# Head sums by column halves, 64x64 products on four quadrants, and new distances in an RWKV-7 recurrence

## The chip, the cores and the metric

The kernel runs on one NeuronCore of one Trainium2 chip. Its time is the time on the device in microseconds (us); three runs are summed up by their median. The core's engines work on their own and wait for each other by semaphores: TensorE (PE) multiplies matrices, VectorE (DVE) and ScalarE (ACT) do elementwise work, GpSimd (POOL) a little of it, and SyncE (SP) issues most DMAs. PE reads from SBUF, which has 128 partitions, and writes to PSUM. PSUM has eight banks here, each of 128 partitions by 512 fp32 numbers; DVE or ACT must empty a bank before it is used again. A product takes its weights from partitions (the rows of PE's array) and leaves its result on partitions that belong to the array's columns. A product of 64x64 weights uses one quadrant of the array: a row half, given by the partition half of its inputs, and a column half, given by the partition half of its output.

## What is computed

One layer of a decoder: 1024 tokens of width 1024, all in float32. Cut to what the change touches:

```python
h = rms_norm(x)
z = h @ W_in
A = dilated_window_attention(q, k, v)          # 8 heads x 64
R = rwkv7(r, k, v, ...)                        # 8 heads x 64
x = x + rms_norm(concat[A, R] @ W_out)
x = x + rms_norm(relu(rms_norm(x) @ W_up)**2 @ W_down)

# in rwkv7, for each head
kk = k * k_k
kk = kk / max(sqrt(sum(kk * kk)), 1e-12)       # sum over the 64 numbers of a head
b = kk * a
for t in range(1024):
    sa = state @ kk[t]
    state = state * w[t] - outer(sa, b[t]) + outer(v[t], k[t])
    y[t] = state @ r[t]
bonus = sum(r * k * r_k) * v                   # sum over a head again
out = (group_norm(y) + bonus) * g
```

## The kernel before

The recurrence is worked in chunks of 64 tokens, so that most of it becomes products. Eight heads are four pairs, p = 0 to 3; a pair's two heads lie on the two partition halves (`own[0]`, `own[1]`). Sixteen chunks are handled as two halves f of eight. Inside a chunk the state's update is a triangular system, and its inverse is built per pair:

- `norms` (L379) sums the squares of each head of k: `pst`, eight products per pair of a 128x128 tile with `bone`, the two columns that mark the heads.
- `pre_pair` (L400) spreads the norms (`pn`, transposes), scales by the decay (`kk`, `ar`, `bk`, `km`), and forms the products `pN` of bk and ar (L433 to L436), one bank of tag "w" for each f. One DVE multiply by a mask empties it into N (L437). `pb` (L453) sums the bonus over heads, in the form of `pst`. The diagonal 16x16 blocks of N go through DRAM.
- `subst` (L478) inverts these blocks on DVE.
- `merge` (L496) combines them to 64x64 in two steps. Step one: `qu1` = N times X, copied to W by ACT (L511), then `qu2` = W times Z, copied into Z by DVE where a mask says so (L519), and a transpose (L520). Each of the two is 32 products per pair. Step two, `qu3` and `qu4`, does the like with 32x32 products.

Then eight units n of two chunks each run through all heads: `unit_ab` (products p of tag "w" and transposes ptk, banks "a" and "b"), `unit_e` (E, banks "a" and "b"), and `unit_c`, the loop over chunks that can't be broken. There, O gets 16 products with the state HV, ACT copies VU out of O (L635), O gets 16 products with VU, DVE adds HV (L641) and scales it for the next chunk (L642). `unit_g` is the group norm and gate of a unit; its operand bv comes by DMA.

Beside these run the input projections, tiles z_*: three matmuls per step, 24 steps for each half of a slab of 128 columns. Those of attention's last pair (z_aq, z_ak and z_av of p = 3) are allowed only after "C7", the recurrence's end. `gate` computes g (three matmuls, then an ACT copy), eight tiles that also use tag "w".

What sets the order: the planner `drive` runs while the program is built. Each job is a generator that, step by step, yields (PE cost, delay, label, needs). The planner's clock `now` counts PE cost. When a job's delay is over and its needs are met, its step is emitted; when no job is due, one filler step of three projection matmuls is emitted, at 0.7. The table `WAIT` (L31) overrides the delay of a job's start or of one of its steps by name (`mrg0.0` is the first step of merge of pair 0, `pre1.2` the third of pre_pair of pair 1, and so on). The order of PE and of SP is fixed by what comes out; the order on ACT and DVE is chosen by a scheduler by priorities and readiness. After the recurrence follow attention, W_out and the FFN.

The helpers that the change uses: `mm` is one matmul, and `mm_h` two, by column halves of the weights:

```python
for s_ in range(2):
    last = mm(o[64 * s_:64 * s_ + 64], lhsT[:, 64 * s_:64 * s_ + 64], rhs, start, stop)
```

## Time and profile before

| what | value |
|---|---|
| runs | 1335.83, 1336.62, 1343.36 us |
| median | 1336.62 us |
| span of the profiled execution | 1340.4 us |
| PE busy | 1279.0 us |
| DVE busy | 905.0 us |
| ACT busy | 625.9 us |
| recurrence's preparation and units on PE | about 80 to 440 us of the span |

The profiled execution has no time of its own beside its span; the span lies 3.8 us above the median. PE is the busiest engine over the whole span. In the rows of a timeline a number is the start, the next the duration of a group of equal instructions; what stands in brackets is the idle time of that engine ahead of it and what ended that. In the rows of stretches come the stretch, its length, the busy time of each engine with its count of instructions, the granted clock of PE (1.00 is full), and the share and rate of DMA. The granted clock is a measured number of the trace.

### The profile page before, as it was taken

What the parts mean: (1) busy time and instruction counts of PE and PEld (TensorE: products, weight loads), DVE (VectorE), ACT (ScalarE), POOL (GpSimd) and SP (SyncE); (2) the same over time, 40 slices, a digit from 0 to 9 for tenths busy, and PEclk for the clock granted to TensorE, in tenths of its full rate; (3) what the DMA queues carried; (4) which work ended last, traced back from release to release, by engine and by line L of the source; (5) the groups of instructions that cost most, each with busy time, mean ns of one, the idle gap of its engine ahead of it and who ended that gap; (6) DMA issues with size and microseconds to landing.
All of it is one profiled execution on the core that took longest, in us unless ns stands there. A gap on an engine that the chain in (4) does not pass through costs nothing.

```text
span 1340.4 us, 23558 instructions
## 1 busy us (share of the span) xinstructions
PE 1279.0 (95%) x9360; PEld 1057.7 (79%) x9360; DVE 905.0 (68%) x1647; ACT 625.9 (47%) x1026; POOL 36.2 (3%) x56
## 2 busy tenths in 40 slices
PE   6899999999889979999998999999999999999997
PEld 5687888888777868787886888888888888888875
DVE  7867668632778457554889977667766775446586
ACT  7653334233545267664656443434444444443442
POOL 0000000000000000000000000000000002000210
PEclk9999999999989989999999999999999999999999
DMA  7346756976774686503434454454457984345564
GB/s 259 116 173 174 189 138 170 257 206 215 218 233 150 204 249 189 139 25 96 142 109 143 171 171 146 141 165 156 151 182 246 348 321 166 95 140 191 188 211 166
DMA packets 163757, 239.48 MB, mean 179 GB/s; under 512 B 52192, under 2 KB 89312, under 8 KB 163648
## 3 DMA queue, kind: packets, MB, share of 16 engines
q1 hardware_dynamic: 154304, 212.81, 50.5%
q10 hardware_dynamic: 8064, 20.98, 4.6%
q0 software_dynamic: 1280, 4.20, 0.8%
q8 instruction: 73, 1.20, 0.4%
q14 instruction: 36, 0.29, 0.1%
HBM read 160.85 MB, written 77.09 MB: 178 GB/s over the span
## 4 chain that ended last, share of the span: by engine, by line
PE 75%; DVE 10%; DMA 7%; ACT 4%; issue 2%; SPq 1%; DVEq 0%; ACTq 0%
PE X L47 12%; PE dX L47 9%; PE Z L47 6%; PE pm L47 5%; PE dZ L47 5%; PE dY L47 3%; PE z_aq L47 3%; PE Y L47 3%; PE z_r L47 3%; PE z_v L47 3%; PE z_k L47 3%; PE z_av L47 3%; PE z_ak L47 2%; PE pS L47 2%; PE pT L908 2%
## 5 line engine op out<-in xcount | busy, mean ns | idle before, releaser
L47 PE MATMUL dX<-wow,wou 128*128 128x512 f32 x768 | 175.9, 390 | 2.7 <-DVE wow L1178 2.2
L47 PEld LDWEIGHTS dX<-wow,wou 128*128 128x128 f32 x768 | 143.8, 188 | 34.1 <-DVE wow L1178 3.5
L47 PE MATMUL dZ<-wow,wou 128*128 128x512 f32 x384 | 87.4, 389 | 0.0
L1177 ACT ACTIVATE wow<-wd 128x1024 fp32r<-128x1024 f32 x40 | 42.3, 1059 | 89.7 <-PE dZ L47 29.8
L47 PEld LDWEIGHTS dZ<-wow,wou 128*128 128x128 f32 x384 | 72.1, 188 | 15.0
L1178 DVE TENSOR_TENSOR wou<-ur,wou 128x1024 fp32r<-128x1024 f32 x56 | 72.0, 1287 | 6.9 <-ACT wou L1177 6.7
L1178 DVE TENSOR_TENSOR wow<-wd,wow 128x1024 fp32r<-128x1024 f32 x40 | 49.9, 1250 | 35.0 <-ACT wow L1177 34.8
L1177 ACT ACTIVATE wou<-ur 128x1024 fp32r<-128x1024 f32 x56 | 58.5, 1049 | 19.8 <-DMA ur<-u_d 12.4
L896 DVE CUSTOM_DVE_ANT_0 S<-pS,stripT 128x512 f32<-128x512 f32 (+3 forms) x64 | 37.6, 588 | 38.7 <-PE pS L47 19.7
L898 ACT ACTIVATE S<-S,mn 128x128 f32<-128x128 f32 (+7 forms) x64 | 49.3, 771 | 19.7 <-DVE mn L896 19.1
L1265 ACT ACTIVATE r<-u 128x512 f32<-128x512 f32 x48 | 30.0, 626 | 51.4 <-DVE u L1263 51.0
L908 PE MATMUL pT<-cst,S 128*128 128x128 f32 x288 | 43.7, 278 | 8.3 <-ACT PT L910 5.4
L47 PE MATMUL pm<-WO,mxr 128*128 128x512 f32 x192 | 49.1, 400 | 0.8 <-DVE mxr L976 0.8
L47 PE MATMUL pm<-WO,mxa 128*128 128x512 f32 x192 | 47.3, 403 | 0.0
L1178 DVE TENSOR_TENSOR wow<-TK,wow 128x1024 fp32r<-128x1024 f32 x16 | 20.8, 1301 | 38.9 <-ACT wow L1177 38.9
L47 PE MATMUL Z<-HB,wo 128*128 128x512 f32 x192 | 46.1, 389 | 0.0
L47 PE MATMUL z_aq<-hT,wh_aq 128*128 128x512 f32 x128 | 45.5, 407 | 0.0
L47 PE MATMUL X<-HB,wo 128*128 128x512 f32 x180 | 43.6, 390 | 1.6 <-ACT HB L1038 1.6
L47 PE MATMUL z_av<-hT,wh_av 128*128 128x512 f32 x128 | 45.2, 409 | 0.0
L908 PEld LDWEIGHTS pT<-cst,S 128*128 128x128 f32 x288 | 32.4, 140 | 16.0 <-ACT PT L910 10.5
L47 PE MATMUL z_k<-hT,wh_k 128*128 128x512 f32 x128 | 42.6, 395 | 1.4 <-DVE z L234 1.4
L47 PE MATMUL z_ak<-hT,wh_ak 128*128 128x512 f32 x128 | 43.7, 404 | 0.0
(388 smaller groups left out, 3060.6 us busy)
## 6 DMA issues: line engine op xcount, KB each, us to landing
ur<-u_d SPq DMA_DIRECT2D x56, 512.0 KB, 4.4
wd<-in_wdown_dram SPq DMA_DIRECT2D x40, 512.0 KB, 4.3
u_d<-S SPq DMA_DIRECT2D x64, 256.0 KB, 2.0
u_d<-u SPq DMA_DIRECT2D x48, 256.0 KB, 2.1
wr_upa<-in_wup_dram SPq DMA_DIRECT2D x16, 512.0 KB, 3.6
wr_upb<-in_wup_dram SPq DMA_DIRECT2D x16, 512.0 KB, 4.0
TK<-in_wdown_dram SPq DMA_DIRECT2D x16, 512.0 KB, 7.1
x<-in_x_dram SPq DMA_DIRECT2D x8, 512.0 KB, 7.0
```

What stands on the lines that cost most here:

```text
L47: return PE.matmul(o, lhsT, rhs, start=start, stop=stop, skip_group_check=True)
L896: V.tensor_tensor_reduce(Sx[:, lo:hi], pS[:, :hi - lo], stripT[:, so:so + hi - lo], 1.0, 3e38 if k == 0 else mn[:, 0:1], OP.add, OP.min, a ...
L898: A.activation(Sx[:, :w], Sx[:, :w], AF.Exp, scale=-1.0, bias=mn[:, nbk - 1:nbk], accum_out=at[p, "den"][:, i, h:h + 1])
L908: PE.transpose(pt[:, j], Sx[:, (4 * k + j) * P:(4 * k + j + 1) * P], ident)
L1177: A.activation(w[:, 0, 0:n], raw, AF.Copy)
L1178: E.tensor_tensor(w[:, 1, 0:n], raw, w[:, 0, 0:n].bitcast(F32), OP.subtract)
L1265: A.activation(r, src, AF.Relu)
```

## The change

It has three parts. First, the head sums `pst` and `pb` are computed by column halves (`mm_h`): 16 products of 128x64 weights per pair in place of 8 of 128x128. Second, the 64x64 products `pN`, `qu1` and `qu2` go to four quadrants by the new helper `turned`: results of even chunks stay on the partition half of their inputs (bank r = 0), those of odd chunks go to the other half (bank r = 1). The number of products stays. Each step's banks are now divided by the parity of the chunk instead of by f; `pN` takes both banks of tag "w" for each f, where it took one. The results are brought back to their places on the way out of PSUM (`sides`), by three operations: one for the even chunks, one for each half of the odd ones. Third, the steps' costs and delays in the planner and the table `WAIT` are set anew, so the order on PE and SP changes.

```diff
-WAIT = {'mrg1.0': 26.0, 'mrg1.3': 4.0, ..., 'vo0_1': 18.5, ..., 'VU3': 5.5, ..., 'EO1_1': 1, ...}
+WAIT = {'mrg1.0': 26.0, 'mrg1.3': 4.5, ..., 'vo0_1': 12.5, ..., 'VU3': 8.0, ..., 'EO1_1': 5.0, ..., 'norm0': 0, ..., 'pre0.2': 1.0, ...}
 ...
-                    mm(pst[:, 8 * f + 2 * t:8 * f + 2 * t + 2], sq[:, t * P:(t + 1) * P], bone)
+                    mm_h(pst[:, 8 * f + 2 * t:8 * f + 2 * t + 2], sq[:, t * P:(t + 1) * P], bone)
 ...
-            yield 2.0, 4.0
+            yield 1.2, 4.0
+
+        sides = [(slice(0, P), slice(0, P), 0), (lo, hi, 1), (hi, lo, 1)]
+
+        def turned(pq, f, lhsT, rhs):
+
+            for cc in range(0, 8, 2):
+                for r in range(2):
+                    for h in range(2):
+                        mm(pq[r][own[h ^ r], 4 * f + cc // 2], lhsT[own[h], cc + r], rhs[own[h], cc + r])
 ...
-                pN = bank(f"pN{p}_{f}", "w", bufs=2)
-                for cc in range(8):
-                    for h in range(2):
-                        mm(pN[own[h], cc], bk[own[h], cc, 0, :], ar[own[h], cc, 0, :])
-                V.tensor_tensor(N[:, 8 * f:8 * f + 8], pN, maskn.unsqueeze(1).to_broadcast([P, 8, 64]), OP.mult)
-                yield 1.0, (3.0, 2.5)[f]
+                pN = [bank(f"pN{p}_{f}_{r}", "w", (P, 4, 64), 2) for r in range(2)]
+                turned(pN, 0, bk[:, :, 0], ar[:, :, 0])
+                Nf = N[:, 8 * f:8 * f + 8]
+                for d, s_, r in sides:
+                    V.tensor_tensor(Nf[d, r::2], pN[r][s_], maskn[s_].unsqueeze(1).to_broadcast([s_.stop - s_.start, 4, 64]), OP.mult)
+                yield 0.7, (3.2, 2.7)[f]
 ...
-                    mm(pb[:, 8 * f + 2 * t:8 * f + 2 * t + 2], T[f][3][:, t * P:(t + 1) * P], bone)
+                    mm_h(pb[:, 8 * f + 2 * t:8 * f + 2 * t + 2], T[f][3][:, t * P:(t + 1) * P], bone)
             V.tensor_copy(BON[:, :, p, :], pb[:, 0:16].rearrange("p (t h) -> p t h", h=2))
-            yield 1.8, 1.0, f"B{p}"
+            yield 1.1, 1.0, f"B{p}"
 ...
+            pq = [bank(f"qu1_{p}_{r}", "bc"[r]) for r in range(2)]
             for f in range(2):
-                fs = slice(8 * f, 8 * f + 8)
-                pu = bank(f"qu1_{p}_{f}", "bc"[f])
-                for cc in range(8):
-                    for h in (0, 64):
-                        mm(pu[h:h + 64, cc], N[h:h + 64, 8 * f + cc], X[h:h + 64, 8 * f + cc])
-                A.activation(W[:, fs], pu, AF.Copy)
-            yield 2.4, 1.5
+                turned(pq, f, N[:, 8 * f:8 * f + 8], X[:, 8 * f:8 * f + 8])
+            for d, s_, r in sides:
+                A.activation(W[d, r::2], pq[r][s_], AF.Copy)
+            yield 1.3, 2.6
+            pq = [bank(f"qu2_{p}_{r}", "bc"[r]) for r in range(2)]
 ...
+                turned(pq, f, W[:, 8 * f:8 * f + 8], Z[:, 8 * f:8 * f + 8])
+            for d, s_, r in sides:
+                V.copy_predicated(Z[d, r::2], mk32[d].unsqueeze(1).to_broadcast([d.stop - d.start, 8, 64]), pq[r][s_])
             V.transpose(fl(X), fl(Z))
-            yield 2.4, 4.0
+            yield 1.3, 4.7
```

How the order moves, at three places. A row has the line, the operation, the output and its inputs with their numbers, the size of one instruction, and how many follow each other.

The first place is PE in the preparation of pair 0, where its first state products pN stand (g is a tile of the gate, z_r filler, pst belongs to pair 1). Before:

```order
L47 MATMUL g_964<-ghl,sgs 128x512 x3
L47 MATMUL z_r_0_897<-hT,wh_r_754 128x512
L47 MATMUL z_r_0_897<-hT,wl_r_755 128x512
L47 MATMUL z_r_0_897<-hT,wh_r_754 128x512
L47 MATMUL g_974<-ghl,sgs 128x512 x3
L47 MATMUL pN_0_997<-ar_0_992,bk_0_993 64x64 x16
L47 MATMUL g_1015<-ghl,sgs 128x512 x3
L47 MATMUL z_r_0_897<-hT,wh_r_754 128x512
L47 MATMUL z_r_0_897<-hT,wl_r_755 128x512
L47 MATMUL z_r_0_897<-hT,wh_r_754 128x512 x2
```

After, from the last products of pN's first half to the first of its second half:

```order
L47 MATMUL pN_0_1_967<-ar_0_961,bk_0_962 64x64 x2
L47 MATMUL pst_987<-cst,sq_0_988 64x2 x8
L47 MATMUL pst_987<-cst,sq_1_998 64x2 x8
L47 MATMUL g_1024<-ghl,sgs 128x512 x3
L47 MATMUL z_r_0_926<-hT,wh_r_754 128x512
L47 MATMUL z_r_0_926<-hT,wl_r_755 128x512
L47 MATMUL z_r_0_926<-hT,wh_r_754 128x512
L47 MATMUL g_1034<-ghl,sgs 128x512 x3
L47 MATMUL pN_1_0_1048<-ar_1_1043,bk_1_1044 64x64 x2
L47 MATMUL pN_1_1_1049<-ar_1_1043,bk_1_1044 64x64 x2
```

Before, g_1015 behind pN took the bank that ACT had emptied, as pN held one of the two banks of tag "w". Now pN holds both, pst has moved behind it, and g_1024 takes a bank that DVE must empty of pN; pN of the second half follows the next g at once.

The second place is DVE around the operation that empties this pN. Before, the multiply stands here:

```order
L451 TENSOR_TENSOR bk_0_993<-km_0_1086,in_0_809 128x8x64
L91 SCALAR_TENSOR_TENSOR n_1_939<-rsm_kk_942,n_1_939 128x16
L446 TENSOR_TENSOR ar_1_1045<-ev_r_1_748,P_1_986 128x8x64
L89 TENSOR_TENSOR rsm_kk_942<-n_1_939 128x16
L449 TENSOR_TENSOR km_1_1094<-km_1_1094,ev_k_1_633 128x512
L90 SCALAR_TENSOR_TENSOR rsm_kk_942<-rsm_kk_942,n_1_938 128x16
L437 TENSOR_TENSOR N_981<-pN_0_997,cst 128x512
L91 SCALAR_TENSOR_TENSOR n_1_939<-rsm_kk_942,n_1_939 128x16
L450 SCALAR_TENSOR_TENSOR ev_r_1_748<-ev_r_1_748,par,km_1_1094 128x512
```

After, the three operations stand here:

```order
L459 SCALAR_TENSOR_TENSOR ev_r_0_688<-ev_r_0_688,par,km_0_1084 128x512
L460 TENSOR_TENSOR bk_0_962<-km_0_1084,in_0_846 128x8x64
L458 TENSOR_TENSOR km_1_1092<-km_1_1092,ev_k_1_633 128x512
L737 TENSOR_TENSOR wl_v_922<-wr_v_919,wh_v_921 128x512
L459 SCALAR_TENSOR_TENSOR ev_r_1_748<-ev_r_1_748,par,km_1_1092 128x512
L460 TENSOR_TENSOR bk_1_1044<-km_1_1092,in_1_847 128x8x64
L737 TENSOR_TENSOR wl_v_922<-wr_v_919,wh_v_921 128x512
L446 TENSOR_TENSOR N_950<-pN_0_0_966,cst 128x4x64
L390 TENSOR_SCALAR n_1_1008<-pst_987 128x16
L446 TENSOR_TENSOR N_950<-pN_0_1_967,cst 64x4x64
L86 TENSOR_SCALAR rsi_kk_1011<-n_1_1008 128x16
L446 TENSOR_TENSOR N_950<-pN_0_1_967,cst 64x4x64
```

Between kk of pair 0 and the first N multiply there are now 18 large operations and one small, among them two for the weights of v (wl_v); the small ones of pair 1's norms have moved behind it.

The third place is PE in the last unit, n = 7 (HV and VU are its state and its update, T and TR its matrices; z_av and z_aq are filler, z_aq of the kind that waits for the recurrence's end). Before:

```order
L47 MATMUL O_1_4758<-VU_4496,TR_1025 64x64 x16
L47 MATMUL E_1_4839<-TR_1026,Zp_4499 64x128 x8
L47 MATMUL z_av_0_4689<-hT,wh_av_4082 128x512
L47 MATMUL z_av_0_4689<-hT,wl_av_4083 128x512
L47 MATMUL z_av_0_4689<-hT,wh_av_4082 128x512 x2
L47 MATMUL z_av_0_4689<-hT,wl_av_4083 128x512
L47 MATMUL z_av_0_4689<-hT,wh_av_4082 128x512
L47 MATMUL O_0_4860<-HV_4683,T_7_4649 64x64 x16
L47 MATMUL z_av_1_4877<-hT,wh_av_4082 128x512
L47 MATMUL z_av_1_4877<-hT,wl_av_4083 128x512
L47 MATMUL z_av_1_4877<-hT,wh_av_4082 128x512 x2
L47 MATMUL z_av_1_4877<-hT,wl_av_4083 128x512
```

After:

```order
L47 MATMUL O_1_4886<-HV_4626,T_6_4574 64x64 x16
L47 MATMUL E_0_4905<-TR_1070,Zp_4632 64x128 x8
L47 MATMUL z_av_1_4712<-hT,wh_av_3841 128x512
L47 MATMUL z_av_1_4712<-hT,wl_av_3842 128x512
L47 MATMUL z_av_1_4712<-hT,wh_av_3841 128x512
L47 MATMUL O_1_4886<-VU_4629,TR_1069 64x64 x16
L47 MATMUL E_1_4972<-TR_1070,Zp_4632 64x128 x8
L47 MATMUL O_0_4985<-HV_4832,T_7_4780 64x64 x16
L47 MATMUL O_0_4985<-VU_4835,TR_1070 64x64 x16
L47 MATMUL O_1_5026<-HV_4832,T_7_4780 64x64 x16
L47 MATMUL O_1_5026<-VU_4835,TR_1070 64x64 x16
L47 MATMUL z_aq_0_5100<-hT,wh_aq_5088 128x512
```

Before, six to nine products of filler stood between the groups of O; now the filler ends ahead of unit 7's groups, and z_aq follows the last of them.

## The prediction

> **What bounds the kernel now.** I read the page first, then the busy time by stretches of the stage that the change touches, then TensorE's timeline there.

> ```profile
> span 1340.4 us, 23558 instructions
> PE 1279.0 (95%) x9360; PEld 1057.7 (79%) x9360; DVE 905.0 (68%) x1647; ACT 625.9 (47%) x1026; POOL 36.2 (3%) x56
> ...
> PE 75%; DVE 10%; DMA 7%; ACT 4%; issue 2%; SPq 1%; DVEq 0%; ACTq 0%
> ```

> TensorE (PE) is busy 95% of the span and holds 75% of the chain that ended last. The stage from 80 to 440 us is more one-sided still:

> ```profile
> core 0: us, PE busy (x) PEld busy (x) DVE busy (x) ACT busy (x) POOL busy (x), PEclk, DMA share, GB/s
> 200.00:250.00 50.00, 50.00 (x629) 41.37 (x629) 38.42 (x75) 18.69 (x33) 1.16 (x3) 1.00 0.67 183
> ...
> 400.00:450.00 50.00, 48.75 (x635) 39.12 (x636) 39.92 (x100) 23.21 (x39) 1.08 (x2) 1.00 0.47 147
> ```

> From 200 to 250 us PE never stops, while DVE works 38 and ACT 19 of 50 us; from 400 on PE misses 1.25 us in 50. So each microsecond of PE work removed there shortens the span, if nothing makes PE wait instead. The filler products (tiles z_) fill every gap that the planner foresees, and their number is fixed. The end of the stage:

> ```profile
> 438.60 1.15 PE L47 MATMUL O<-VU,TR 128*64 128x64 f32 x32
> 439.68 0.50 PE L47 MATMUL z_av<-hT,wh_av 128*128 128x512 f32 x1
> ...
> 440.49 0.39 PE L47 MATMUL z_aq<-hT,wh_aq 128*128 128x512 f32 x1
> ```

> The recurrence's last group, O from VU, takes 1.08 us to the start of the next product at 439.68; its filler (z_av) ends at 440.5. They run out together. The z_aq behind them waited in the planner for the recurrence's end. Hence time that the recurrence saves is gained whole, but work brought forward to fill early gaps is missing at the end.

> **Shorter products.** Each fp32 product leaves two records. I take start-to-start times, from a group to the next one.

> ```profile
> 81.71 1.84 PE L47 MATMUL pst<-cst,sq 128*128 128x2 f32 x16
> 83.41 0.96 PE L47 MATMUL g<-ghl,sgs 128*128 128x512 f32 x3
> ...
> 95.18 1.15 PE L47 MATMUL pN<-ar,bk 64*64 64x64 f32 x32
> 96.26 0.97 PE L47 MATMUL g<-ghl,sgs 128*128 128x512 f32 x3
> ...
> 154.92 2.08 PE L47 MATMUL qu<-X,N 64*64 64x64 f32 x64
> 156.93 0.50 PE L47 MATMUL z_k<-hT,wh_k 128*128 128x512 f32 x1
> ...
> 165.52 1.20 PE L47 MATMUL qu<-X,N 32*32 32x32 f32 x64
> 166.65 0.50 PE L47 MATMUL z_k<-hT,wh_k 128*128 128x512 f32 x1
> ...
> 321.40 1.09 PE L47 MATMUL E<-TR,Zp 64*64 64x128 f32 x16
> 322.42 0.50 PE L47 MATMUL z_av<-hT,wh_av 128*128 128x512 f32 x1
> ```

> pst takes 1.70 us for 16 records. Split into column halves it becomes 32 records of 128x64 weights, the form of the O group above, which takes 1.08. pst and pb occur once for each of four pairs: 8 x (1.70 - 1.08) = 5.0 us. Bounds: 0, if halves that stream only two columns do not overlap, and 5.0.

> pN takes 1.08 for 32 records, qu1 and qu2 2.01 for 64: by their difference 29.1 ns a record and 0.15 us a group. These rows run on two row halves. O and E run on two column halves; E streams different data through one row half, and at 128 columns its record costs 1.02/16 = 64 ns, about twice a 64-column one's 29.1, so its column halves overlap too. Both splits together, four quadrants, appear nowhere. If all four overlap, a record costs half, 14.6 ns; the 32x32 row shows that records can follow so fast (1.13 us for 64, that is 0.15 + 64 x 15.3 ns). I take 15.3: pN 8 x (1.08 - 0.64) = 3.5 us, qu1 and qu2 8 x (2.01 - 1.13) = 7.0. Bounds for both: 0 (still two at a time) and 10.5. Together these terms give 15.5 us, within 0 to 15.5. I take the upper end, because each split alone overlaps in its rows.

> [...]

> **More evacuations.** Since odd chunks come out on the other partition half, a half pair's pN is emptied by three DVE operations instead of one, a pair's qu2 by three instead of two, and its qu1 by three instead of two on ACT.

> ```profile
> 98.79 0.68 DVE L437 TENSOR_TENSOR N<-pN,cst 128x512 f32<-128x512 f32 x1
> ...
> 160.40 0.74 DVE L519 COPY_PREDICATED Z<-mk,qu 128x512 f32<-128x512 int32 x1 [0.17 <-PE qu L47]
> ```

> The new pieces of pN hold half as many columns; at about 0.4 each (an estimate from 0.68) they add 8 x 0.5 = 4 us of DVE work, and Z four times 0.74. W adds as much on ACT. In the stretches above DVE idles 10 us in 50, and the new distances in the planner, 2.6 from qu1 to qu2 and 4.7 from qu2 to qu3, cover three copies of which the first two run beside the products. I cost this at 0; without that cover it is 4 x 0.74 twice, 6 us.

> **Waits that go.**

> ```profile
> 125.97 1.15 PE L47 MATMUL pN<-ar,bk 64*64 64x64 f32 x32 [1.57 <-DVE bk L432]
> ...
> 390.63 1.97 PE L47 MATMUL O<-HV,T 128*64 128x64 f32 x32 [3.46 <-DVE HV L642]
> ...
> 423.20 1.15 PE L47 MATMUL O<-HV,T 128*64 128x64 f32 x32 [0.69 <-DVE HV L642]
> ```

> The first stands before pair 1's state products: by the new order 13 us of PE work lie between pn and pN there, for a DVE chain of under 10. The last (unit 6) now has products of unit 7 and nine fillers in front. Both go: -2.3 us. Units 2 to 5 keep their order, so the middle one stays. Bounds: 0, and -5.8 if that goes too.

> **Waits that come.** First, pair 0. pN now takes both banks of tag w, which the g products need too. g after pst can start only when DVE has emptied pN's even bank, and DVE has 18 large operations and a small one between pn and that.

> ```profile
> 87.64 1.03 PE L411 MATMUL pn<-cst,nb 128*128 128x128 f32 x8
> 88.28 1.40 DVE L426 SCALAR_TENSOR_TENSOR kk<-ev_k,par,pn 128x512 f32<-128x512 f32 x2 [0.25 <-PE pn L411]
> ...
> 88.43 0.94 PE L47 MATMUL g<-ghl,sgs 128*128 128x512 f32 x3
> ...
> 91.60 0.93 PE L47 MATMUL g<-ghl,sgs 128*128 128x512 f32 x3
> ...
> 92.55 0.68 DVE L430 TENSOR_TENSOR ar<-kk,P 128x512 f32<-128x512 f32 x1
> 93.05 0.84 PE L47 MATMUL g<-ghl,sgs 128*128 128x512 f32 x3
> 93.15 0.17 DVE L87 TENSOR_SCALAR n<-rsi_kk 128x16 int32<-128x16 int32 x1
> ```

> DVE begins 0.64 after pn; with 0.60 us to the next operation (92.55 to 93.15), and 0.07 more for each of the five that are longer and for the small one, it takes 11.2, and the multiply 0.4: 12.25 us after pn starts. PE arrives after pn (0.79), five times three g and three z (1.45 each, 91.60 to 93.05), pN (0.64) and pst (1.08), that is 9.75. It waits 2.5; then pN of the second half waits about 0.65 for ACT's copy of the g before it: +3.2. Bounds: 0, if DVE runs its small and large operations closer, and 4.

> Second, the last unit. All filler is spent before it; before, 27 filler products stood between its groups. Now VU (0.59 on ACT), HV and its multiply lie bare:

> ```profile
> 433.64 0.50 PE L47 MATMUL z_av<-hT,wh_av 128*128 128x512 f32 x1
> ...
> 435.00 0.68 DVE L642 TENSOR_TENSOR HV<-HV,PcL 64x512 f32<-64x512 f32 x1
> ...
> 437.01 0.50 PE L47 MATMUL z_av<-hT,wh_av 128*128 128x512 f32 x1
> 437.12 0.59 ACT L635 ACTIVATE VU<-O 64x512 f32<-64x512 f32 x1 [1.53 <-PE O L47]
> ```

> The z_av at 433.64 and 437.01 mark the ends of the O groups ahead of them. HV is ready at 435.68, about 2.1 us after its O group; E covers 1.02 of that once; VU is ready at 437.71, some 0.75 after O, twice; the second HV costs 1.7 to 2.1: 1.1 + 0.75 + 1.8 + 0.75 = 4.4. Bounds: 3.3 (DVE at once) and 6 (group norm in front on DVE).

> Third, units 0 and 1: E directly behind the transposes waits for ACT, and masks stand in front of HV on DVE.

> ```profile
> 335.96 0.71 PE L580 MATMUL ptk<-cst,K 64*128 64x64 f32 x15 [0.53 <-ACT TR L599]
> ```

> That wait grows by about 0.7, and two HV waits of 0.4 each join: +1.5, bounds 0 and 3. SP's one load more is issued with the queue idle and nobody waits for it. Attention and everything behind keep their order, with as many z_aq fillers ahead; their waits move with them: 0.

> **The sum.** -15.5 - 2.3 + 3.2 + 4.4 + 1.5 = -8.7 us. The profiled execution's span of 1340.4 becomes 1331.7; it lies 3.8 above the median of 1336.6, so against the median I predict 1328.

> **Rivals.**

> *The new waits do not appear* (DVE and ACT are sooner than I count, PE stays the bound throughout): -15.5 - 2.3 = -17.8, or about -16 with one small wait, hence 1319 to 1321. For it: the stretches without any PE idle. Against it: the last unit has no filler in its order at all, so only the first and third wait can be gone altogether.

> *The clock.* After PE idles, its granted clock falls:

> ```profile
> core 0: us, PE busy (x), PEclk, DMA share, GB/s
> 125.00:130.00 5.00, 4.04 (x45) 1.00 0.50 87
> 388.00:392.00 4.00, 1.37 (x26) 0.83 0.97 264
> 392.00:396.00 4.00, 4.00 (x31) 0.50 0.42 153
> ```

> The 3.46 us wait was followed by 4 us at 0.50; O's records took 1.97 there, against 1.15 elsewhere: 2 to 3 us lost. The 1.57 us wait left the clock at 1.00. The new waits are 2.5 and, in pieces, 4.4 and 1.5, between the two. One event gives 1331, two 1334, three 1337.

> *Quadrants do not overlap by four*, so the change does not do what it says. Place: pN, qu1, qu2. Two at a time as now, 10.5 us stay: -8.7 + 10.5 = +1.8, or 1338. One at a time, 768 records (256 of pN, 512 of qu) at 58 ns instead of 29.1 add 22: 1361, the side of slower. It decides from the point where a record exceeds 29.1 - 1.8/0.768 = 26.8 ns; from there on the new waits outweigh the rest. For it: no row shows four. Against: E and pN, above. [...]

> **How the numbers follow.** A measurement of this kernel can tell about 1% from no change, here 1323 and 1350. Forecast, 1323 to 1333: 0.48. No new waits, about 1320: 0.26. Clock events, 1331 to 1337: 0.12. Two quadrants at a time, 1335 to 1338: 0.10; one at a time or a further wait of this size, above 1350: 0.04. Faster by over 1% is the second case and a little of the forecast's low end, 0.30; slower 0.04; the rest, 0.66, is within 1%. The range runs from 1318 (nothing of the new waits and all gains) to 1338 (two quadrants at a time).

> **What would show it.** Groups: pst and pb at 1.1 instead of 1.70 us, pN near 0.64, qu1 and qu2 near 1.13. No idle before pair 1's first pN. In pair 0 an idle of about 2.5 us before a g, released by DVE's N multiply. In the last unit about 4.4 us in four pieces, released by HV and VU. The third wait of unit 4 still near 3.5. The last O from VU ending near 431 instead of 439.7, and the same distance from there to the end. It is wrong if pN stays at 29 ns a record, if the clock shows 0.5 after the new waits, or if the end does not follow the recurrence's.

## The result and the profile after

The changed kernel took 1349.59 us (median of 4 runs, 1347.76 to 1351.59), the kernel before in the same comparison 1338.83 us. The ratio is 1.0062, with a 95% interval from 1.0034 to 1.0091: 0.6% slower, some 8 to 11 us, where about 9 us faster were forecast.

The page of the changed kernel: its span, the engines' busy time, and the chain that ended last.

```profile
span 1347.0 us, 23854 instructions
...
PE 1273.1 (95%) x9488; PEld 1047.3 (78%) x9488; DVE 915.5 (68%) x1667; ACT 628.4 (47%) x1030; POOL 36.5 (3%) x56
...
PE 68%; DVE 14%; DMA 10%; ACT 4%; issue 3%; SPq 1%; DVEq 0%; ACTq 0%
```

PE is busy 5.9 us less than before (the same work counts longer where the clock is lower: an O group 1.15 us at full clock, 1.97 at 0.50), and the span is 6.6 us longer. The recurrence's last group, O from VU, starts at 437.24 us of the span (shown below), against 438.60 before; the distance from there to the end, which the prediction kept, grew from 901.8 to 909.7 us. PE's part of the chain fell from 75% to 68%; DVE's rose from 10% to 14%, DMA's from 7% to 10%. PE now waits for others more often.

First the products. The timeline of PE in the changed kernel, with start, duration, and how many records:

```profile
102.80 1.10 PE L47 MATMUL pb<-cst,ev_r 128*64 128x2 f32 x32
103.83 0.51 PE L47 MATMUL z_r<-hT,wh_r 128*128 128x512 f32 x1
...
124.46 0.69 PE L47 MATMUL pN<-ar,bk 64*64 64x64 f32 x32
125.08 0.50 PE L47 MATMUL z_k<-hT,wh_k 128*128 128x512 f32 x1
...
152.98 1.16 PE L47 MATMUL qu<-X,N 64*64 64x64 f32 x64
154.07 0.50 PE L47 MATMUL z_k<-hT,wh_k 128*128 128x512 f32 x1
```

From start to start, pb takes 1.03 us (1.70 before), pN 0.62 (1.08), qu1 1.09 (2.01). Times 8 groups each that is 5.4 + 3.7 + 7.4 = 16.5 us less PE work. The products did all that the change is about.

Where it went, by stages. For each profiled execution the table gives the length of three stages on PE: from 75 us to the first E (preparation), from there to the start of the last O of VU (units), and from there to the first X, a product of the FFN (attention, with W_out). Behind them stand PE's idle time in the three stages, and the time lost to a lower clock: the sum over stretches of 4 us of (1 - granted clock) x length. The lower rows belong to the experiments below; in them the first column names the kernel, and the ratio is that of its own comparison. The stages are those of one execution each; that of halves_pN took 8 us less than the kernel's median, the others lie within 5 us of theirs.

| kernel | preparation | units | attention | idle | lost to clock | ratio to before |
|---|---|---|---|---|---|---|
| before | 246.4 | 117.2 | 273.2 | 29.1 | 10.2 | 1 |
| changed | 247.4 | 114.8 | 280.9 | 42.6 | 18.8 | 1.0062 |
| halves | 239.5 | 116.1 | 273.3 | 25.4 | 10.3 | 0.9964 |
| halves_qu | 239.1 | 118.0 | 270.6 | 33.1 | 6.8 | 0.9955 |
| halves_pN | 252.2 | 111.3 | 269.4 | 33.7 | 6.8 | 1.0051 |
| quads | 258.4 | 118.5 | 273.1 | 41.9 | 20.4 | 1.0117 |
| newcode_oldplan | 252.4 | 115.8 | 270.4 | 41.1 | 13.6 | 1.0050 |
| oldcode_newplan | 258.9 | 112.9 | 277.0 | 35.3 | 17.1 | 1.0090 |
| after_qu | 251.2 | 116.8 | 281.7 | 48.3 | 23.8 | 1.0123 |
| after_c5 | 250.8 | 119.8 | 284.8 | 59.0 | 22.1 | 1.0142 |
| after_lead27 | 248.1 | 114.4 | 276.0 | 41.8 | 15.3 | 1.0018 |
| halves_lead29 | 239.8 | 116.6 | 276.8 | 29.1 | 10.2 | 0.9990 |
| after_pNold | 244.2 | 115.8 | 279.4 | 38.4 | 17.1 | 1.0009 |
| halves_qu_wait27 | 242.5 | 123.0 | 275.5 | 38.8 | 17.1 | 1.0005 |
| halves_pN_pieces | 246.9 | 118.2 | 271.1 | 28.1 | 13.6 | 0.9999 |
| halves_pN_banks | 250.1 | 119.0 | 270.8 | 32.3 | 13.6 | 1.0040 |
| after_pNold_lead27 | 243.8 | 116.4 | 274.9 | 35.8 | 15.4 | 0.9987 |

Changed against before: products -16.5, idle +13.5, clock +8.6, sum +5.6 us, against +6.6 between the spans. So the question is where the waits come from, and why the clock falls. One number more is counted in the programs' order: ahead of the first E stand 962 filler products before and 992 after, ahead of the last O of unit 7 1109 and 1112. The changed plan spends 30 filler products more (6.8 us) in the preparation, and 27 of them are missing in the units.

The largest waits of PE in the changed kernel's preparation and units, in brackets the idle time and what ended it:

```profile
97.58 0.96 PE L47 MATMUL g<-ghl,sgs 128*128 128x512 f32 x3 [1.21 <-DVE N L446]
...
100.60 0.68 PE L47 MATMUL pN<-ar,bk 64*64 64x64 f32 x28 [0.42 <-ACT go L354]
...
210.59 1.20 PE L47 MATMUL qu<-X,N 32*32 32x32 f32 x64 [1.62 <-DVE X L525]
...
251.46 1.20 PE L47 MATMUL qu<-X,N 32*32 32x32 f32 x64 [1.61 <-DVE X L525]
...
362.10 1.67 PE L47 MATMUL O<-HV,T 128*64 128x64 f32 x32 [2.94 <-DVE HV L647]
...
429.71 1.15 PE L47 MATMUL O<-HV,T 128*64 128x64 f32 x32 [1.30 <-DVE HV L647]
...
431.54 1.15 PE L47 MATMUL O<-VU,TR 128*64 128x64 f32 x32 [0.68 <-ACT VU L640]
...
434.58 1.97 PE L47 MATMUL O<-HV,T 128*64 128x64 f32 x32 [1.89 <-issue]
...
437.24 1.97 PE L47 MATMUL O<-VU,TR 128*64 128x64 f32 x32 [0.68 <-ACT VU L640]
```

The first two are pair 0's wait for the banks of tag w. The next two, before qu3 of pairs 1 and 2, were not in the forecast, nor was the fifth, in unit 2. The last four are the last unit without filler; its last two O groups run at a granted clock of 0.50 (1.97 us for 1.15). For the wait of 1.89 us the profile names no releaser.

Behind the three waits that were not forecast stands the same thing. DVE in the changed kernel:

```profile
204.71 0.69 DVE L455 TENSOR_TENSOR ar<-ev_r,P 128x512 f32<-128x512 f32 x1 [1.33 <-DMA ar_d<-ar]
...
209.20 1.25 DVE L525 STREAM_TRANSPOSE X<-Z 128x1024 f32<-128x1024 f32 x1
...
248.23 0.18 DVE L485 COPY Zt<-G 128x15 f32<-128x15 f32 x1 [1.33 <-DMA G<-n_d]
...
250.08 1.24 DVE L525 STREAM_TRANSPOSE X<-Z 128x1024 f32<-128x1024 f32 x1
...
357.42 0.69 DVE L670 TENSOR_TENSOR bv<-bv,BON 128x512 f32<-128x512 f32 x1 [4.39 <-DMA bv<-v_d]
...
361.36 0.68 DVE L647 TENSOR_TENSOR HV<-HV,PcL 64x512 f32<-64x512 f32 x1
```

DVE is not busy with too much work there. It stands idle for a DMA (1.33, 1.33 and 4.39 us), and what PE needs (qu2's copies with the transpose X, or HV) comes later in its order. In the kernel before, a wait of DVE for the same kind of load, bv, of 1.63 us, stands ahead of PE's wait of 3.46 us in unit 4.

### The profile page after: what moved, and what is told of

It reads as the page before. It is cut to its first block, busy times and chain, and to the rows that moved or that the text cites. A ratio compares the mean times of both kernels' runs of the same rounds, so it can differ in the third digit from the quotient of the medians.

```text
span 1347.0 us, 23854 instructions
## 1 busy us (share of the span) xinstructions
PE 1273.1 (95%) x9488; PEld 1047.3 (78%) x9488; DVE 915.5 (68%) x1667; ACT 628.4 (47%) x1030; POOL 36.5 (3%) x56
## 4 chain that ended last, share of the span: by engine, by line
PE 68%; DVE 14%; DMA 10%; ACT 4%; issue 3%; SPq 1%; DVEq 0%; ACTq 0%
PE X L47 12%; PE dX L47 9%; PE Z L47 6%; PE pm L47 6%; PE dZ L47 5%; PE dY L47 3%; PE Y L47 3%; PE pS L47 3%; PE z_ak L47 2%; PE z_av L47 2%; PE pT L913 2%; PE z_aq L47 2%; PE z_r L47 2%; PE po L47 2%; PE z_k L47 2%
## 5 line engine op out<-in xcount | busy, mean ns | idle before, releaser
L47 PE MATMUL dX<-wow,wou 128*128 128x512 f32 x768 | 176.0, 390 | 2.3 <-DVE wow L1183 1.5
L47 PEld LDWEIGHTS dX<-wow,wou 128*128 128x128 f32 x768 | 143.8, 188 | 33.8 <-DVE wow L1183 2.8
L47 PE MATMUL dZ<-wow,wou 128*128 128x512 f32 x384 | 87.4, 389 | 0.0
L47 PEld LDWEIGHTS dZ<-wow,wou 128*128 128x128 f32 x384 | 72.1, 188 | 15.0
L47 PE MATMUL pm<-WO,mxr 128*128 128x512 f32 x192 | 49.8, 404 | 0.8 <-DVE mxr L981 0.8
L47 PE MATMUL pm<-WO,mxa 128*128 128x512 f32 x192 | 47.0, 402 | 0.0
L47 PE MATMUL Z<-HB,wo 128*128 128x512 f32 x192 | 46.1, 389 | 0.0
L47 PE MATMUL z_ak<-hT,wh_ak 128*128 128x512 f32 x128 | 45.5, 416 | 0.0
L47 PE MATMUL X<-HB,wo 128*128 128x512 f32 x180 | 43.6, 390 | 1.6 <-ACT HB L1043 1.6
L47 PE MATMUL z_aq<-hT,wh_aq 128*128 128x512 f32 x128 | 45.1, 410 | 0.0
L47 PE MATMUL z_k<-hT,wh_k 128*128 128x512 f32 x128 | 43.1, 396 | 1.4 <-DVE z L234 1.4
L47 PE MATMUL z_av<-hT,wh_av 128*128 128x512 f32 x128 | 44.1, 406 | 0.0
```

Source lines behind the costliest of these rows:

```text
L47: return PE.matmul(o, lhsT, rhs, start=start, stop=stop, skip_group_check=True)
```

## The experiments

Each kernel was compared with the kernel before, on the same chip, in five rounds. Differences between two kernels below come from their two ratios; with the intervals of both they are good to 3 to 6 us.

**Code against plan.** Four kernels part the change: head sums by column halves alone; quadrants alone; both under the planner's costs, delays and table of before; the old products under the new costs, delays and table.

halves (the same two edits in pst and pb, nothing else):

```diff
-                    mm(pst[:, 8 * f + 2 * t:8 * f + 2 * t + 2], sq[:, t * P:(t + 1) * P], bone)
+                    mm_h(pst[:, 8 * f + 2 * t:8 * f + 2 * t + 2], sq[:, t * P:(t + 1) * P], bone)
```

> The kernel before with the head sums pst and pb by column halves alone; planner costs, delays and table as before, so PE's order stays row for row but for these products. Theory (the products gain what their rows say and the plan loses it): 8 groups x (1.70 - 1.02) = 5.4 us faster, ratio about 0.996, attention and the rest unchanged. Rival (time saved in the recurrence is lost again in attention, whatever saved it): no faster than before, within 2 us.

Ratio 0.9964 (0.9946 to 0.9982), 4.8 us: as the theory had it.

quads (pN, qu1 and qu2 as in the change; pst, pb, yields and WAIT of before):

```diff
+                turned(pN, 0, bk[:, :, 0], ar[:, :, 0])
 ...
+                turned(pq, f, N[:, 8 * f:8 * f + 8], X[:, 8 * f:8 * f + 8])
```

> The kernel before with pN, qu1 and qu2 on four quadrants and their three evacuations, head sums, costs, delays and table as before. Theory: products save 8 x (1.08 - 0.64) + 8 x (2.01 - 1.08) = 10.9 us; up to 5 us come back as waits for the third evacuation, since the planner still counts 2.4 for a qu; 6 to 11 us faster, ratio 0.992 to 0.995. Rival (the extra evacuations cost what the products save): within 2 us of before.

Ratio 1.0117 (1.0093 to 1.0141): 16 us slower, further out than either theory. The preparation grew by 12 us.

newcode_oldplan (the changed kernel with all costs, delays and the table as before; one of the lines):

```diff
-            yield 1.3, 4.7
+            yield 2.4, 4.0
```

> The changed code in full (halves and quadrants) with the costs, delays and the table of before, so PE, ACT and DVE keep the old order in attention and the last unit keeps its 27 filler products. Theory (the plan loses it): 12 to 16 us faster than before, about 1324, ratio 0.988 to 0.991. Rival (the code itself brings the waits): 1345 to 1352, as the changed kernel.

Ratio 1.0050 (1.0027 to 1.0073), median 1349.63: in the rival's range. The plan alone is not to blame: under the old one the code is slow as well.

oldcode_newplan (the kernel before with the new yields and the new WAIT; the same line):

```diff
-            yield 2.4, 4.0
+            yield 1.3, 4.7
```

> The products of before (full head sums, two row halves, one bank a half) under the new costs, delays and table. Theory (the plan loses it): slower than the changed kernel by some of the 16 us of products, less what longer products cover of its waits: 1355 to 1365. Rival (the code brings the waits): about as before, 1335 to 1342.

Ratio 1.0090 (1.0064 to 1.0117), median 1353.13: a little under the range that the theory gave, and far from the rival's. Both code and plan cost something. The code costs in the preparation: under the old plan it takes 6.0 us longer there than before, with products that are 16.5 us shorter. The plan costs in attention (277.0 and 280.9 us with the new plan, 269 to 273 with the old); with the old products, for which its costs and delays were not made, it also costs 8.2 us in preparation and units together.

**Which quadrants.** halves_qu has the halves and quadrants in qu1 and qu2 only, halves_pN the halves and quadrants in pN only, both under the plan of before. The edit of halves_qu, against newcode_oldplan (cut):

```diff
-                pN = [bank(f"pN{p}_{f}_{r}", "w", (P, 4, 64), 2) for r in range(2)]
-                turned(pN, 0, bk[:, :, 0], ar[:, :, 0])
+                pN = bank(f"pN{p}_{f}", "w", bufs=2)
 ...
```

> Head sums by halves, qu1 and qu2 on four quadrants with three evacuations, pN as before; costs, delays and table of before. Theory (the third evacuation ends after the planner's distance, and each wait is followed by a stretch at a lower clock): against the kernel with halves alone 7.4 us less PE work, but about 6.5 us of waits before qu2 and qu3 and some 5 us of lower clock, so 2 to 6 us slower than halves alone, ratio to before 0.998 to 1.002. Rival (only pN, which takes both banks of tag w, does harm): 5 to 8 us faster than halves alone, ratio 0.991 to 0.993.

Ratio 0.9955 (0.9938 to 0.9971), the fastest of all kernels here. Against halves alone it gains about 1 us of the 7.4, which the intervals don't separate, so it lies between the two theories: waits take the rest, but no lower clock followed them in the preparation. Its two longest for qu:

```profile
156.58 1.15 PE L47 MATMUL qu<-Z,W 64*64 64x64 f32 x60 [1.61 <-ACT W L518]
...
244.96 1.20 PE L47 MATMUL qu<-X,N 32*32 32x32 f32 x64 [1.21 <-DVE tmp L490]
```

In pair 0, ACT's last copy of W lets PE go on only 1.61 us after PE has come to qu2.

> Head sums by halves, pN on four quadrants over both banks of tag w, qu1 and qu2 as before; costs, delays and table of before. Theory: 3.5 us less PE work than halves alone, about 6.5 us of waits for DVE's evacuation before g and before the next pN and some 3 us of lower clock, so 4 to 8 us slower than halves alone, ratio 0.999 to 1.003. Rival (only qu does harm): 2 to 4 us faster than halves alone, ratio 0.993 to 0.995.

Ratio 1.0051 (1.0031 to 1.0072), 11 to 12 us slower than halves alone, more than the 4 to 8 of the theory. pN is the harm, with products that are 3.7 us shorter. What it waits for:

```profile
99.85 1.65 PE L47 MATMUL g<-ghl,sgs 128*128 128x512 f32 x3 [3.51 <-DVE N L446]
...
189.54 0.33 PE L47 MATMUL pN<-ar,bk 64*64 64x64 f32 x4 [1.94 <-DVE N L446]
```

**The second bank or the extra evacuations.** Two kernels part them, on the halves kernel and without quadrants; the one with two banks can't do without one extra evacuation. halves_pN_pieces empties pN's one bank in three operations:

```diff
-                V.tensor_tensor(N[:, 8 * f:8 * f + 8], pN, maskn.unsqueeze(1).to_broadcast([P, 8, 64]), OP.mult)
+                Nf = N[:, 8 * f:8 * f + 8]
+                for d, r in ((slice(0, P), 0), (lo, 1), (hi, 1)):
+                    V.tensor_tensor(Nf[d, r::2], pN[d, r::2], maskn[d].unsqueeze(1).to_broadcast([d.stop - d.start, 4, 64]), OP.mult)
```

> Head sums by halves; pN's products and its one bank as before, but emptied by three DVE operations (even chunks, and each half of the odd ones) in place of one; plan of before. If the extra evacuations are what makes pN on quadrants dear: 6 to 12 us slower than halves alone, ratio to before 1.001 to 1.006. If the second bank is: within 2 us of halves alone, ratio 0.995 to 0.998.

Ratio 0.9999 (0.9980 to 1.0019): some 4.7 us slower than halves, between the two expectations.

halves_pN_banks puts even and odd chunks into two banks and empties each with one operation:

```diff
-                pN = bank(f"pN{p}_{f}", "w", bufs=2)
+                pN = [bank(f"pN{p}_{f}_{r}", "w", (P, 4, 64), 2) for r in range(2)]
 ...
-                        mm(pN[own[h], cc], bk[own[h], cc, 0, :], ar[own[h], cc, 0, :])
+                        mm(pN[cc % 2][own[h], cc // 2], bk[own[h], cc, 0, :], ar[own[h], cc, 0, :])
```

> Head sums by halves; pN's products on two row halves as before, but even and odd chunks into the two banks of tag w, emptied by one DVE operation each (two in place of one, of half the size); plan of before. If the second bank is what makes pN dear: 6 to 12 us slower than halves alone, ratio to before 1.001 to 1.006, with waits for DVE's evacuation before g and before the next pN. If the extra evacuations are: ratio 0.995 to 0.999.

Ratio 1.0040 (1.0019 to 1.0060): 10 us slower than halves, as expected of the bank. The waits, first of the kernel with two banks:

```profile
99.76 1.65 PE L47 MATMUL g<-ghl,sgs 128*128 128x512 f32 x3 [3.14 <-DVE N L439]
...
187.72 1.36 PE L47 MATMUL pN<-ar,bk 64*64 64x64 f32 x32 [1.48 <-DVE N L439]
```

and of the kernel with three pieces:

```profile
139.23 0.50 PE L47 MATMUL z_r<-hT,wl_r 128*128 128x512 f32 x1 [2.11 <-DVE wl_r L734]
```

The bank, with the one extra operation that it brings, is the larger cause: g and the next pN wait for it. The pieces cost through other work that DVE does later for them: here wl_r, the low half of a filler's weights. In the kernel with two banks an undisturbed pN group still takes 1.08 us, so it is the quadrants that shorten it to 0.62, not the second bank.

**The same in the changed kernel.** after_pNold is the changed kernel with pN as before, plan as changed.

```diff
-                turned(pN, 0, bk[:, :, 0], ar[:, :, 0])
+                for cc in range(8):
+                    for h in range(2):
+                        mm(pN[own[h], cc], bk[own[h], cc, 0, :], ar[own[h], cc, 0, :])
```

> The changed kernel with pN as before: one bank, two row halves, one multiply; plan as changed. Theory (under the changed plan pN's wait in pair 0 is small): 3.5 us more PE work against 1.6 us of waits less, within 3 us of the changed kernel, 1347 to 1353. Rival (both banks of tag w are what makes the changed kernel slow, as under the plan of before): 8 to 13 us faster, 1337 to 1342.

Ratio 1.0009 (0.9992 to 1.0027): 7 us faster than the changed kernel (3.9 between the two profiled executions), a little short of the rival's 8 to 13. The theory falls: it put pN's harm at the 1.6 us of pair 0's waits. But the two waits before qu3 are gone too, and in this execution the lower clock in the preparation (3.4 us lost in the changed kernel, none here). DVE comes to the same two operations without a wait:

```profile
203.85 0.69 DVE L455 TENSOR_TENSOR ar<-ev_r,P 128x512 f32<-128x512 f32 x1
...
246.21 0.16 DVE L485 COPY Zt<-G 128x15 f32<-128x15 f32 x1
```

So pN reaches as far as qu3, by way of the DMAs: N is stored (n_d), the load of G waits for that store, and the stores ar_d stand behind it in SP's order. In pair 2, N's last piece ends 5.4 us after pN's second half began, against 3.5 us here. In the changed kernel the pieces and the second bank were not parted, and how much of the delay is the DMAs' own is open. The wait in unit 2 stays (2.83 us), so it is not pN's.

**Filler.** after_qu gives qu2 to qu3 more distance in pairs 1 and 2, where the 1.6 us waits are.

```diff
-'mrg1.2': 5.0, ..., 'mrg2.2': 4, ...
+'mrg1.2': 8.0, ..., 'mrg2.2': 7.0, ...
```

> The changed kernel with two distances in the table made longer, from qu2 to qu3 of pair 1 (5.0 to 8.0) and of pair 2 (4.0 to 7.0); the two waits of 1.6 us there should go. Theory (the filler is short, so a wait that is filled in the preparation comes back in the last units): within 3 us of the changed kernel, 1346 to 1353. Rival (those waits and the lower clock behind them are simply lost): 5 to 7 us faster, 1343 to 1345.

Ratio 1.0123 (1.0101 to 1.0145): slower by another 8 us, which neither expected. The two waits are gone, but one of 2.65 us for DVE stands at another place of the preparation, 15 filler products more (1007) lie ahead of the first E, and the preparation is 3.8 us longer. The units have these 15 products fewer, and the time lost to the clock there is 10.1 us, against 3.3 in the changed kernel.

after_c5 lets the fillers of attention's last pair start early, so that the last unit has them:

```diff
-        ..., False, "C7" if p == 3 else None) ...
+        ..., False, "C5" if p == 3 else None) ...
```

> The changed kernel with the slabs of attention's last pair allowed after the sixth unit instead of after the recurrence, so the last unit has 30 more filler products in its order, taken from the stretch ahead of attention. Theory (what the shorter products save is missing as filler at the end): the last unit's waits of 4.5 us and the half clock behind them go, 3 to 7 us faster than the changed kernel, 1343 to 1347, if the start of attention does not wait longer. Rival (filler does not matter, attention waits for its loads instead): 1348 to 1352.

Ratio 1.0142 (1.0107 to 1.0178), median 1360.82: slower than both expectations. In the last unit the waits fall from 4.6 to 2.4 us, and the half clock there goes (0.50 in the changed kernel, 1.00 here). But the fillers were needed at attention's start, where they had covered its loads:

```profile
484.10 0.45 PE L47 MATMUL pS<-kh,qs 128*128 128x128 f32 x1 [10.58 <-DMA kh<-qk_d]
...
490.37 0.48 PE L47 MATMUL pS<-kl,qs 128*128 128x128 f32 x1 [5.82 <-DMA kl<-qk_d]
...
498.59 0.80 PE L47 MATMUL pS<-kh,qs 128*128 128x512 f32 x1 [7.74 <-DVE mn L901]
```

halves_qu_wait27 lengthens two distances of halves_qu, and begins attention three filler products earlier, to keep its order:

```diff
+'mrg0.1': 3.0, 'mrg2.2': 5.0
 ...
-        LEAD = 28
+        LEAD = 27
```

> Head sums by halves and qu on quadrants, pN as before, plan of before with two longer distances (qu1 to qu2 of pair 0 3.0 for 1.5, qu2 to qu3 of pair 2 5.0 for 4.0) and attention begun three filler products earlier, so that its order stays nearly that of before. Theory (filler is what counts): the waits of 1.6 and 1.2 us in the preparation go, and about as much comes back in the last unit, whose last step has no filler; within 3 us of the kernel with halves and qu, ratio to before 0.994 to 0.998. Rival: 3 to 6 us faster than it, ratio 0.991 to 0.993.

Ratio 1.0005 (0.9988 to 1.0022), 6 to 7 us slower than halves_qu, worse than both expectations. Again 12 filler products more stand ahead of the first E, the units are 5 us longer, and attention starts with a wait of 4.77 us for its load. In three tries, filling one wait brought others elsewhere, and the kernel became slower.

**The order in attention.** PE's order in attention is fixed, but ACT's and DVE's is chosen by the scheduler, which goes by its own forecast of when things are ready. The changed plan alters it in some 30 rows of DVE's 456. What sets it off is small: the changed kernel has used up three filler products more by the recurrence's end (1112 against 1109), so behind attention's first product 12 are left, before 15. The order can be flipped by starting attention three filler products earlier or later:

```diff
-        LEAD = 28
+        LEAD = 27
```

> The changed kernel with attention begun three filler products earlier (LEAD 27 for 28). The scheduler then gives ACT and DVE in attention the order that they had before the change (one row differs), with the recurrence as in the changed kernel. Theory (a part of the loss is the other order in attention and the lower clock behind its waits): attention shrinks from 281 us to 271 to 275, the kernel is 4 to 8 us faster than the changed one, 1342 to 1346. Rival (attention is slow from what the recurrence leaves behind, whatever the order): within 2 us of the changed kernel, 1348 to 1352.

Ratio 1.0018 (1.0002 to 1.0034), median 1343.95: 6 us faster than the changed kernel, as expected; attention shrinks to 276.0 us, a little less than expected. The mirror, LEAD 29 on the halves kernel:

> The mirror of it: head sums by halves alone, under the plan of before, with attention begun three filler products later (LEAD 29). ACT and DVE in attention then have the changed kernel's order (one row differs). Theory: attention grows from 273 to 277 to 281 us, 4 to 8 us slower than the kernel with halves alone, ratio to before 0.999 to 1.003. Rival: as halves alone, ratio 0.995 to 0.998.

Ratio 0.9990 (0.9970 to 1.0009), 3.5 us slower than halves alone: in the expected direction, but the two intervals overlap. The table says it more clearly. With the changed kernel's order, or nearly it, attention takes 276.8 to 281.7 us in five kernels (changed, oldcode_newplan, after_qu, after_pNold, halves_lead29); in the eight under the old plan with LEAD 28 it takes 269.4 to 273.3; in the three with LEAD 27 it takes 274.9 to 276.0. How it comes about shows on DVE and PE of the changed kernel. WO is a weight of W_out, needed much later; PT's copy is what PE waits for:

```profile
533.68 1.28 DVE L955 SCALAR_TENSOR_TENSOR WO<-wo,par,WO 128x1024 fp32r<-128x1024 f32 x1 [0.32 <-ACT WO L954]
534.88 0.68 DVE L901 CUSTOM_DVE_ANT_0 S<-pS,stripT 128x512 f32<-128x512 f32 x1
...
535.49 0.55 DVE L917 COPY PT<-pT 128x384 f32<-128x384 f32 x1
...
536.19 0.52 PE L913 MATMUL pT<-cst,S 128*128 128x128 f32 x3 [1.36 <-DVE PT L917]
```

In after_lead27 the same WO operation stands behind, and the wait at this place is 0.29 us:

```profile
534.61 0.69 DVE L901 CUSTOM_DVE_ANT_0 S<-pS,stripT 128x512 f32<-128x512 f32 x1
...
535.06 0.66 PE L913 MATMUL pT<-cst,S 128*128 128x128 f32 x4 [0.29 <-ACT PT L915]
...
535.22 1.28 DVE L955 SCALAR_TENSOR_TENSOR WO<-wo,par,WO 128x1024 fp32r<-128x1024 f32 x1
```

What makes it dear is the clock behind such waits: of attention's 7.7 us more, waits are 1.8 and the clock 7.0. The changed kernel, PE by stretches of 4 us (length, busy, granted clock, DMA share, GB/s), around its waits of 1.44, 1.36 and 1.89 us in attention:

```profile
516.00:520.00 4.00, 2.06 (x15) 0.94 0.81 259
520.00:524.00 4.00, 4.00 (x34) 0.63 1.07 265
532.00:536.00 4.00, 2.40 (x15) 1.00 0.02 4
536.00:540.00 4.00, 3.81 (x14) 0.57 0.55 165
591.00:595.00 4.00, 2.11 (x13) 0.95 0.22 68
595.00:599.00 4.00, 4.00 (x24) 0.62 0.00 0
```

**Both causes at once.** after_pNold_lead27 has pN as before and LEAD 27.

```diff
-                turned(pN, 0, bk[:, :, 0], ar[:, :, 0])
+                        mm(pN[own[h], cc], bk[own[h], cc, 0, :], ar[own[h], cc, 0, :])
 ...
-        LEAD = 28
+        LEAD = 27
```

> The changed kernel with pN as before and attention begun three filler products earlier, so that attention has the order of before. If pN (7 us) and the order in attention (6 us) are two separate causes, they add: ratio to before 0.994 to 0.998, about as halves with qu. If they are one, or something else of the plan is at work: ratio 1.000 to 1.003.

Ratio 0.9987 (0.9966 to 1.0008): between the two ranges, 10 us under the changed kernel where the sum of the two is 13. The interval reaches into both ranges, and each difference is good to some 5 us, so it isn't shown whether they add in full. But together pN and the order in attention make up most of the loss. What is left against halves_qu, some 4 us, was not parted further. Its units idle 14.1 us, those of halves_qu 9.1, so the last unit without filler is a candidate, argued and not shown.

## Why the prediction was wrong, step by step

The forecast's terms beside what the two profiled executions show, in us:

| term | forecast | measured |
|---|---|---|
| products | -15.5 | -16.5 |
| waits in the preparation | +1.6 | +6.3 |
| waits in the units | +5.2 | +5.4 |
| waits in attention | 0 | +1.8 |
| lower clock | 0 | +8.6 |
| sum | -8.7 | +5.6 |

So of the miss some 9 us are the clock, which the sum left out, nearly 5 are waits in the preparation, and 2 are waits in attention.

*The products* were right: 15.5 us forecast, 16.5 measured. On four quadrants qu1 takes 17 ns a record (1.09/64), on two row halves it took 31 (2.01/64). Each bank here takes quadrants of both row halves, on different partitions, and the 17 ns were measured so.

*The waits that come* were right for the last unit: it was put at 4.4 us and has 1.30 + 0.68 + 1.89 + 0.68 = 4.6. Pair 0 was put at 3.2 and has 1.6. DVE was as slow as forecast: it emptied the bank 12.7 us after pn began, for a forecast of 12.25. But PE came to it 11.5 us after pn, not 9.75; 1.0 us of this is g waiting for ACT's copies on the way. With the 1.0 us that pst waits for ACT ahead of pn, the place costs 3.7 us, about the forecast, but in good part for other reasons.

The rest of the units came out right by luck. "Units 2 to 5 keep their order, so the middle one stays" did not hold: the wait of unit 4 shrank from 3.46 to 1.43 us, and one of 2.94 in unit 2, for which 0 stood in the sum, took its place. What changed there in the timing of DVE's load of bv was not parted further.

*"I cost this at 0"*, the extra evacuations, is the first step that failed, together with the second bank of tag w, which the prediction priced in pair 0 alone. The two waits before qu3 (3.2 us) hang on them, and in this execution 3.4 us of lower clock; after_pNold, which takes pN's pieces and its second bank away, has neither, and is 7 us faster. The cover that was named, a DVE that idles 10 of 50 us, is an average. The later N sets DMAs back, DVE stands idle for these, and PE waits for what comes behind them in DVE's order.

*"Attention and everything behind keep their order, with as many z_aq fillers ahead; their waits move with them: 0"* is the second. It was true of PE but for one step of three fillers, and false of DVE and ACT: 7.7 us in the profiled executions, of which after_lead27 gives back 4.9, and 6 us by the ratios.

*The clock* is the largest single term, and the sum had nothing for it. As a rival it was right as a mechanism, at 3 us an event, with a chance of 0.12 and up to three events. The event that it was priced from, behind the wait of 3.46 us, is 6.83 us at 0.50 and costs 3.4. The new ones mostly last half as long and cost 1.7 each. The changed kernel lost 18.8 in all, the kernel before 10.2, five times 1.7 more: one in the preparation, four in attention, three of these behind waits of only 1.36, 1.44 and 1.89 us. The prediction's own sign of being wrong, a clock of 0.5 after the new waits, was there, and so was the other, an end that doesn't follow the recurrence's.

*"Hence time that the recurrence saves is gained whole"* is the third step that failed. It holds for the halves, whose edit left the plan alone. Where the plan was stretched to cover later results, the filler that covers it came from a fixed stock: before, that stock ended with the recurrence, and a distance made longer early leaves the end without filler.

The rival on the slower side, quadrants that do not overlap, did not occur. No run shows the 1335 us at which the forecast lets two quadrants at a time begin; the changed kernel showed 17 ns a record in qu1 and 19 in pN (0.62/32), below the 26.8 from which that rival was to decide. The rival of the clock was a part of what happened; none named what set most of it off, the order in attention.

## What to carry to other kernels

When a product becomes cheaper by spreading its results over more banks or other partitions, price the emptying first: under the old plan the second bank of a shared pair cost some 10 us here and the two extra pieces some 5, the products saved 3.7. Follow the emptied result to the DMAs that wait for it, and to what stands behind these in the order of an engine that has to wait for them. A plan that fills one engine's gaps with a fixed amount of other work has only that amount to give; a distance made longer early is a wait later. And where a scheduler orders engines by its own forecast, compare the order of all engines in stages that the change doesn't touch.

## What was not expected of the hardware

```profile
516.11:519.52 3.41, 1.47 (x11) 1.00 0.79 253
519.52:522.93 3.41, 3.41 (x14) 0.50 1.09 286
533.18:536.59 3.41, 1.62 (x11) 1.00 0.20 49
536.59:540.00 3.41, 3.41 (x13) 0.50 0.48 149
```

The wait of 2.12 us in halves_qu falls over two windows, with PE busy for 3.07 and 1.63 us, and the clock stayed at 1.00:

```profile
575.19:578.61 3.42, 3.07 (x21) 1.00 0.10 26
578.61:582.02 3.41, 1.63 (x10) 1.00 0.26 77
582.02:585.43 3.41, 3.41 (x50) 1.00 0.01 2
```

So one window at half clock cost 1.7 us (3.413 x 0.50; the losses in the table are multiples of it, such as 6.8, 10.2, 13.6), and whether a wait of 1 to 2.5 us cost it depended here on where it fell. after_lead27 has the changed kernel's recurrence and waits of 2.30 and 0.96 us before qu3, and lost nothing there; it lost a window behind g's wait of 1.21 us instead. Busy time was not the whole measure: in the kernel before, a window without any idle time (168.79 to 172.20 us), mostly filled with 32x32 products and with pst's of two columns, was followed by one at 0.50 as well.

The windows ahead of a fall were not all idle throughout: in the two that are shown, PE was busy for 1.47 and 1.62 of 3.41 us.
